# A seven-product feed-forward on one Trainium2 core: the second weight sum moved, and three of eleven units given a seventh pair

## The chip, the core and the metric

The kernel runs on one core of a Trainium2 chip. The engines are named as in the profile: PE (TensorE, matrix products), PEld (its weight loads), DVE (VectorE), ACT (ScalarE), POOL (GpSimd) and SP (SyncE, which here only issues DMAs). Every engine runs its own instruction list in order; semaphores tie the lists together. The metric is the device time of one execution in microseconds (us), lower is better.

## The reference

A trunk of two residual layers on 256 tokens of width 2048, in float32: attention and feed-forward, then a gated linear recurrence and feed-forward. The change lies in the two feed-forwards:

```python
def swiglu(h, w_gate, w_up, w_down):
    return (jax.nn.silu(h @ w_gate) * (h @ w_up)) @ w_down

x = x + mixer(rms_norm(x, norm_mix[i]))
x = x + swiglu(rms_norm(x, norm_ffn[i]), ffn_w_gate[i], ffn_w_up[i], ffn_w_down[i])
```

`w_gate` and `w_up` are 2048 x 5632, `w_down` is 5632 x 2048.

## The kernel before

**Split precision.** Each float32 operand is held as two fp32r halves: `hi`, a cast made by ACT, and `lo`, the remainder (the value less `hi`) made by DVE. A product is three matmuls of 512 columns (`product`, lines L323, L324, L326: hi by hi, lo by hi, hi by lo). So every 512 KB of weights that arrives costs ACT one cast and DVE one subtraction before PE can use it. `behind("cast", ...)` and `behind("rest", ...)` tie all these casts on ACT and all remainders on DVE into the order in which the program wrote them.

**Units and pairs.** A feed-forward is cut into 11 units of 512 hidden features. In a unit the 2048 rows of `w_gate` and `w_up` come as eight **pairs**, each of 256 rows (two blocks of 128) of gate and of up. A pair is a 2 x 2 block product: tokens in two halves, rows in two blocks, gate and up as the two columns. It is done either plainly, by `load_half` twice and `wide` (8 products, 24 matmuls), or by **seven products** (`load_seven`, 21 matmuls), which needs sums of weight blocks: with b11, b21 (gate) and b12, b22 (up), t1 = b11 + b12, t2 = t1 + b22, t3 = t2 - b11, t4 = t2 + b21. t1 is made by an accumulating DMA on POOL's queue (L176), or on DVE (L174) where three plain loads went ahead; the others are made on DVE (L169) and cast and subtracted in turn (L170, L171). The sums are made in place: t2 over b22, t3 over b11, t4 over b21. The token side needs such sums as well; `Norm.form` makes them once for each feed-forward and each pair that any unit does by seven products.

`SEVEN` names the six pairs so treated (0, 1, 2, 4, 5, 6, counted from 0); `FEWER` gives the first three units fewer. The texts count units and pairs from 1: usually pairs 1, 2, 3, 5, 6, 7 are done by seven products, pairs 4 and 8 plainly. After each of the units 3 to 10 come two column groups of the down projection of an earlier part, 96 matmuls, in `wide_project`; ACT takes their sums out of PSUM with a scale (`form`, L818, the **scaled copies**), and POOL adds them to the residual stream by DMA.

**What sets the order.** PE's order is the program's. The order on DVE, ACT, POOL and SP is made by a list scheduler within the ties that `behind`, `follow`, `ahead` and `held` add. At a unit's end DVE combines the PSUM banks (`sums`, L770 to L773, and L791, L794), ACT applies SiLU, DVE multiplies (L795) and transposes in 32 x 32 blocks (L408), and ACT puts the blocks in their place (L416, sixteen copies). These **turn copies** are split into four lots of four, held in the list `tail`; each `load_seven` of the next unit pops one lot between the casts of its loaded weights and those of its sums. The last lot brings the cast and remainder of the finished features (`whole`, L801 and L802). `parted` ties the second group's scaled copies behind the sums' casts.

**Buffers.** Weight tiles go round 8 `raw` buffers (`landing`), their halves round 7 `hi` and 7 `lo` buffers (`parts`); `ohi` and `olo`, the halves of t2, have two buffers each.

Of the kernel before, what the change touches and what calls it, by code (L numbers as in the profile page):

```python
# [12 lines left out]
F32 = mybir.dt.float32  # L13
F32R = mybir.dt.float32r
AF = mybir.ActivationFunctionType
ALU = mybir.AluOpType
AX = mybir.AxisListType

P = 128
# [8 lines left out]
PARTS = [8, 8, 8, 8, 12]  # L28
UNIT = 4
SEVEN = (0, 1, 2, 4, 5, 6)  # L30
FEWER = {0: (0, 5, 6), 1: (4, 5, 6), 2: (1, 4, 5, 6)}
HALF = 8
CHUNK = HALF * P
WIDE = 512
RING = 5
MORE = 2
RAWS = 3
SCRATCH = 8192
NW = D // WIDE
COMMON = {"ssq", "nm", "nr", "rsq_s"}  # L40
EPS = 1e-6
# [19 lines left out]
PK = {}  # L61
# [13 lines left out]
def trunk(ctx, tc, w, out):  # L75
    nc = tc.nc
    act, dve, pool, pe, sync = nc.scalar, nc.vector, nc.gpsimd, nc.tensor, nc.sync

    cst = ctx.enter_context(tc.tile_pool(name="cst", bufs=1))
# [13 lines left out]
    def tmp(tag, shape=(P, S), dt=F32, bufs=2):  # L93
        pl = tp if tag in COMMON else scope[-1]
        return pl.tile(list(shape), dt, tag=tag, name=nm(tag), bufs=bufs)


    newest = {}

    def follow(i, j):  # L100
        tc.add_manual_dep(
            i.ins, j.ins.name,
            mybir.DependencyInfo(mybir.DependencyClass.NoSync, mybir.DependencyReason.DATA),
            reason="order",
        )


    ring, held, ft, ahead, tail, parted = [0], [], [], [], [], []

    def parts(shape):  # L110
        n = ring[0] = (ring[0] + 1) % (RING + MORE)
        if ft and n >= RING:
            return [scope[-1].tile(shape, F32R, tag="x" + t, name=nm(t), bufs=MORE) for t in ("hi", "lo")]
        return [wp.tile(shape, F32R, tag=t, name=nm(t), bufs=RING) for t in ("hi", "lo")]
# [39 lines left out]
    def load_seven(srcs, soon):  # L154
        raw = [landing([P, 2, WIDE]) for _ in range(2)]
        for r, src in zip(raw, srcs):
            sync.dma_start(out=r, in_=src)
        (b11, b21), (t1, b22) = ([r[:, j, :] for j in range(2)] for r in raw)
        got = {}

        def two(src, names):
            hi, lo = parts([P, 2, WIDE])
            behind("cast", act.copy(hi, src))  # L163
            behind("rest", dve.tensor_tensor(lo, src, hi[:].bitcast(F32), ALU.subtract))  # L164
            for j, name in enumerate(names):
                got[name] = hi[:, j, :], lo[:, j, :]

        def combine(o, x, y, op, hi, lo):
            behind("rest", dve.tensor_tensor(o, x, y, op))  # L169
            behind("cast", act.copy(hi, o))  # L170
            return lambda: behind("rest", dve.tensor_tensor(lo, o, hi.bitcast(F32), ALU.subtract))  # L171

        if soon:
            behind("rest", dve.tensor_tensor(t1, b11, t1, ALU.add))  # L174
        else:
            pool.dma_start(out=t1, in_=b11, accum_op=ALU.add)  # L176
        two(raw[0], ("b11", "b21"))
        two(raw[1], ("t1", "b22"))
        if tail:
            tail.pop(0)()  # L180
        one = [tmp(t, (P, WIDE), F32R) for t in ("ohi", "olo")]
        hi, lo = parts([P, 2, WIDE])
        got["t2"] = tuple(one)
        got["t3"], got["t4"] = ((hi[:, j, :], lo[:, j, :]) for j in range(2))
        t2 = b22
        rests = [
            combine(t2, t1, b22, ALU.add, *got["t2"]),
            combine(b11, t2, b11, ALU.subtract, *got["t3"]),
            combine(b21, t2, b21, ALU.add, *got["t4"]),
        ]  # L190
        while parted:
            follow(parted.pop(), newest["cast"])
        for rest in rests:
            rest()
        return got
# [34 lines left out]
    for b in range(-1, NBLK):  # L230
        xin = range(2 * b + 2, 2 * b + 4) if b + 1 < NBLK else []
        yin = range(KT + 2 * b, KT + 2 * b + 2) if b >= 0 else []
        both = [halves(w["w_in"][c]) for c in (*xin, *yin)]
# [33 lines left out]
    def later(delay, fn):  # L267
        waiting.append((clock[0] + delay, fn))
# [117 lines left out]
    pk = cst.tile([P, PKW], F32, tag="pk", name="pk")  # L386
# [2 lines left out]
    scope.append(ap)  # L389
    xq = [ap.tile([P, 4, S], F32, tag=f"xq{k}", name=f"xq{k}", bufs=1) for k in range(KT // 4)]  # L390
    cn = ap.tile([P, 2 * S], F32, tag="cn", name="cn", bufs=1)
    ones = cst.tile([P, P], F32, tag="ones", name="ones")
    act.dma_start(out=pk[:, :PK0], in_=w["pk"][:, :PK0])
    pool.memset(ones, 1.0)
    idle = ps_m.tile([P, P], F32, tag="pm", name=nm("pm"))
# [28 lines left out]
    class Norm:  # L424
# [30 lines left out]
        def turn(self, g, engines):  # L455
            t = turn_blocks(x_tm[:, :, g * WIDE : (g + 1) * WIDE], engines)
            for k in range(4):
                self.scale(t[:, k, :])
            for i in range(2):
                if self.g[0] == "norm_ffn" and 2 * g + i in SEVEN:  # L460
                    self.form(2 * g + i, t[:, 2 * i : 2 * i + 2, :])

        def form(self, c, src):
            v, t = (tmp("form", (P, 2 * S)).rearrange("p (a b) -> p a b", a=n) for n in (2, 4))
            for j in range(2):
                act.activation(v[:, j, :], src[:, j, :], AF.Copy, scale=col(self.g[0], self.g[1] + 2 * c + j))
            (a11, a21), (a12, a22) = ([v[:, j, a * P : (a + 1) * P] for a in range(2)] for j in range(2))
            for i, x, y, op in (
                (0, a21, a22, ALU.subtract), (1, a11, a21, ALU.subtract),
                (2, t[:, 0, :], a11, ALU.subtract), (3, a12, t[:, 2, :], ALU.add),  # L470
            ):
                pool.tensor_tensor(t[:, i, :], x, y, op)
            hi, lo = (tmp(f"f{n}", (P, 4, P), F32R, bufs=len(SEVEN)) for n in "hl")
            act.copy(hi, t)
            dve.tensor_tensor(lo, t, hi[:].bitcast(F32), ALU.subtract)
            self.forms[c] = [(hi[:, i, :], lo[:, i, :]) for i in range(4)]
# [234 lines left out]
    for h in range(NQ):  # L711
        attend(h, project(n0.xs), o_t[h])

    cs = cst.tile([P, 32], F32, tag="cs", name="cs")
    ncs = cst.tile([P, 32], F32, tag="ncs", name="ncs")

    def decay_constants():
        lam = pk[:, PK["lam"] : PK["lam"] + 32]
        e, s, s2, q = (tmp(f"lr{i}", (P, 32), bufs=1) for i in range(4))
        dve.tensor_scalar(s, lam, -1.0, None, ALU.mult)  # L720
        dve.tensor_tensor(e, lam, s, ALU.max)
        table_act(e, e, AF.Exp, scale=-1.0)
        dve.tensor_scalar(s2, e, 2.0, None, ALU.add)
        dve.reciprocal(s2, s2)
        dve.tensor_tensor(e, e, s2, ALU.mult)
        dve.tensor_tensor(s2, e, e, ALU.mult)
        dve.tensor_scalar(q, s2, 2.0 / 15.0, 2.0 / 13.0, ALU.mult, ALU.add)
        for d in (11, 9, 7, 5, 3, 1):
            dve.tensor_tensor(q, q, s2, ALU.mult)
            dve.tensor_scalar(q, q, 2.0 / d, None, ALU.add)  # L730
        dve.tensor_tensor(q, q, e, ALU.mult)
        dve.scalar_tensor_tensor(q, s, 0.0, q, ALU.max, ALU.add)
        dve.tensor_scalar(cs, q, LRU_C, None, ALU.mult)
        dve.tensor_scalar(ncs, q, -LRU_C, None, ALU.mult)
# [15 lines left out]
    def ffn(norm, nxt):  # L750
# [60 lines left out]
        ends = np.cumsum(PARTS) // UNIT  # L811
        for what, i in ffn_plan():
            if what == "unit":
                hid[int(np.searchsorted(ends, i, "right"))] += unit(FEWER.get(i, SEVEN), 0 < i < ends[-1] - 1, (act,) if i < ends[-1] - 1 else (act, dve), i < ends[0])
            else:
                for a, acc in enumerate(wide_project(hid[i[0]], PARTS[i[0]], bank)):
                    t = tmp("form", (P, WIDE))
                    m = act.activation(t, acc, AF.Copy, scale=norm.r[:, a : a + 1])  # L818
                    if i[1] % 2:
                        parted.append(m)  # L820
                    pool.dma_start(out=x_tm[:, a, i[1] * WIDE : (i[1] + 1) * WIDE], in_=t, accum_op=ALU.add)
# [221 lines left out]
```

## Time and profile before

| what | value |
|---|---|
| runs shown, median (lowest to highest) | 1952.95 us (1952.37 to 1953.81), three runs |
| the profiled execution | 1952.89 us, of which the span from first to last instruction is 1951.1 us |
| attention in full run, 120 to 200 us | PE busy 80.00 of 80.00 us, DVE 65.65, ACT 61.27 |
| recurrence in full run, 1000 to 1100 us | PE busy 100.00 of 100.00 us, DVE 93.91, ACT 90.31 |
| second feed-forward, 1600 to 1700 us | PE busy 100.00 of 100.00 us, DVE 97.12, ACT 75.64 |
| last stretch, 1900 to 1952 us | PE busy 46.97 of 52.00 us |

The page's first part gives each engine's busy time over the span. The view by windows cuts this into stretches, so that stages with different limits can be told apart; the number behind "x" is the count of instructions. The view of waits sums, for each engine and line, how long it stood until which other engine released it. The timeline gives start and duration of single instructions; a row with x2 stands for two in succession. The first feed-forward takes about 266 to 904 us of the span, the second about 1263 to 1900 us.

### The profile page before, as it was taken

Reading aid. Unit: us, or ns where it says so; the run is one execution under the profiler, and the core shown is the slowest. Engines: PE = TensorE matmul, PEld = TensorE weight load, DVE = VectorE, ACT = ScalarE, POOL = GpSimd, SP = SyncE. Lnnn points to the kernel's source line nnn. Section 1 sums busy time; section 2 is a strip of 40 time slices with the busy share of each in tenths; the row PEclk is TensorE's granted clock in tenths of the full one; section 3 lists DMA queues with packets and bytes.
Section 4 is the critical chain, followed back from the end, with each engine's and each line's share of the span. In section 5 each row is a group of like instructions: output and inputs, shape, how many; then the busy total and the mean of one; then the engine's idle time right before and its main releaser. Section 6 shows DMA issues by size and latency. Waiting matters only on the chain.

```text
span 1951.1 us, 27630 instructions
## 1 busy us (share of the span) xinstructions
PE 1938.0 (99%) x9224; PEld 1624.0 (83%) x9224; DVE 1768.6 (91%) x2417; ACT 1448.3 (74%) x2358; POOL 401.3 (21%) x497
## 2 busy tenths in 40 slices
PE   9999999999999999999999999999999999999999
PEld 8898888788888888888899998887888888888887
DVE  7878698999999999998799997898999999999993
ACT  7677686777777777777698887866778776787772
POOL 0442250011101111010465450520101111011100
PEclk9999999999999999999999999999999999999999
DMA  8434746698878978787365556555878888788872
GB/s 328 156 127 152 248 158 197 196 272 236 248 233 243 262 240 246 235 244 246 126 223 188 189 164 245 175 194 174 253 236 248 245 248 253 231 246 251 246 257 86
DMA packets 131727, 426.42 MB, mean 219 GB/s; under 512 B 14720, under 2 KB 14976, under 8 KB 131584
## 3 DMA queue, kind: packets, MB, share of 16 engines
q1 hardware_dynamic: 108944, 383.21, 58.0%
q0 software_dynamic: 22496, 41.43, 11.9%
q8 instruction: 72, 1.18, 0.2%
q14 instruction: 71, 0.58, 0.1%
q10 hardware_dynamic: 144, 0.02, 0.0%
HBM read 382.13 MB, written 2.10 MB: 197 GB/s over the span
## 4 chain that ended last, share of the span: by engine, by line
PE 92%; DVE 4%; ACT 1%; issue 1%; DMA 1%; POOL 0%; SPq 0%; ACTq 0%; DVEq 0%; POOLq 0%
PE acc L326 14%; PE acc L323 14%; PE acc L324 14%; PE pm L326 11%; PE pm L323 11%; PE pm L324 11%; PE acc L294 8%; PE acc L292 4%; PE pm L306 1%; PE pm L307 1%; PE pm L305 1%; DVE lo L146 1%; ACT hi L145 1%; DVE lo L164 0%; DMA raw<-in_w_in_dram 0%
## 5 line engine op out<-in xcount | busy, mean ns | idle before, releaser
L146 DVE TENSOR_TENSOR lo<-raw,hi 128x1024 fp32r<-128x1024 f32 (+1 forms) x474 | 574.5, 1240 | 77.1 <-ACT hi L145 75.3
L145 ACT CAST hi<-raw 128x1024 fp32r<-128x1024 f32 (+1 forms) x474 | 478.4, 1045 | 116.5 <-PE acc L324 72.1
L326 PE MATMUL acc<-lo,xg 128*128 128x512 f32 x744 | 290.9, 391 | 2.0 <-DVE lo L146 1.8
L323 PE MATMUL acc<-hi,xg 128*128 128x512 f32 x744 | 290.0, 390 | 0.0
L324 PE MATMUL acc<-hi,xg 128*128 128x512 f32 x744 | 289.6, 389 | 0.0
L164 DVE TENSOR_TENSOR lo<-raw,hi 128x1024 fp32r<-128x1024 f32 x232 | 275.0, 1217 | 6.5 <-ACT hi L163 3.8
L294 PE MATMUL acc<-xg,hi 128*128 128x512 f32 x832 | 271.7, 397 | 0.6 <-ACT hi L145 0.6
L163 ACT CAST hi<-raw 128x1024 fp32r<-128x1024 f32 x232 | 234.6, 1048 | 41.0 <-issue 14.4
L176 POOL DMA_DIRECT2D raw<-raw x90 | 77.7, 863 | 903.9 <-DVE raw L174 369.5
L323 PE MATMUL pm<-hi,act 128*128 128x512 f32 x512 | 199.2, 389 | 0.0
L324 PE MATMUL pm<-hi,act 128*128 128x512 f32 x512 | 199.2, 389 | 0.0
L326 PE MATMUL pm<-lo,act 128*128 128x512 f32 x512 | 199.2, 389 | 0.0
L416 ACT COPY two<-one 32x256 f32<-32x256 f32 x420 | 169.7, 404 | 24.7 <-DVE one L408 16.5
L292 PEld LDWEIGHTS acc<-xg,lo 128*128 128x128 f32 x832 | 156.3, 188 | 35.4 <-DVE lo L146 2.8
L323 PE MATMUL acc<-hi,act 128*128 128x512 f32 x448 | 174.9, 390 | 0.4 <-DVE two L794 0.4
L326 PE MATMUL acc<-lo,act 128*128 128x512 f32 x448 | 174.4, 389 | 0.0
L324 PE MATMUL acc<-hi,act 128*128 128x512 f32 x448 | 174.4, 389 | 0.0
L292 PE MATMUL acc<-xg,lo 128*128 128x256 f32 x832 | 171.8, 281 | 1.2 <-DVE lo L146 1.2
L326 PEld LDWEIGHTS acc<-lo,xg 128*128 128x128 f32 x744 | 139.7, 188 | 34.1 <-DVE lo L146 5.4
L324 PEld LDWEIGHTS acc<-hi,xg 128*128 128x128 f32 x744 | 139.7, 188 | 29.2
L323 PEld LDWEIGHTS acc<-hi,xg 128*128 128x128 f32 x744 | 139.7, 188 | 28.6
L170 ACT CAST hi<-raw 128x512 fp32r<-128x512 f32 x232 | 137.1, 622 | 32.8 <-DVE raw L169 31.8
(221 smaller groups left out, 3852.1 us busy)
## 6 DMA issues: line engine op xcount, KB each, us to landing
raw<-in_w_gate_dram SPq DMA_DIRECT2D x176, 512.0 KB, 4.6
raw<-in_w_up_dram SPq DMA_DIRECT2D x176, 512.0 KB, 5.5
raw<-in_w_down_dram SPq DMA_DIRECT2D x176, 512.0 KB, 4.4
raw<-in_w_in_dram SPq DMA_DIRECT2D x64, 512.0 KB, 4.4
raw<-raw POOLq DMA_DIRECT2D x90, 256.0 KB, 5.8
raw<-in_w_q_dram SPq DMA_DIRECT2D x32, 512.0 KB, 3.8
raw<-in_w_o_dram SPq DMA_DIRECT2D x32, 512.0 KB, 4.2
x<-form POOLq DMA_DIRECT2D x64, 256.0 KB, 6.7
```

Source lines behind the costliest of these rows:

```text
L145: behind("cast", act.copy(hi[:, sl], raw[:, sl]))
L146: behind("rest", dve.tensor_tensor(lo[:, sl], raw[:, sl], hi[:, sl].bitcast(F32), ALU.subtract))
L163: behind("cast", act.copy(hi, src))
L164: behind("rest", dve.tensor_tensor(lo, src, hi[:].bitcast(F32), ALU.subtract))
L170: behind("cast", act.copy(hi, o))
L176: pool.dma_start(out=t1, in_=b11, accum_op=ALU.add)
L292: pe.matmul(acc[:, S:], w, xs[k][:, :S], start=False, stop=stop)
L294: pe.matmul(acc, w, xs[k], start=(k == 0), stop=stop)
L323: pe.matmul(o, xh, wh, start=start, stop=False)
L324: pe.matmul(o, xl, wh, start=False, stop=False)
L326: pe.matmul(o, xh, wl, start=False, stop=stop)
L416: m = (eng.copy if eng is act else eng.tensor_copy)(to[:, :, :, i, :], of[:, :, :, j, :])
```

## The change

The core of the diff; left out are renamed uses and two lines that only follow from it.

```diff
-FEWER = {0: (0, 5, 6), 1: (4, 5, 6), 2: (1, 4, 5, 6)}
+CHOSEN = {0: (0, 5, 6), 1: (4, 5, 6), 2: (1, 4, 5, 6)}
+MANY = tuple(range(7))
+CHOSEN.update({i: MANY for i in (4, 7, 10)})
...
-SCRATCH = 8192
+SCRATCH = 4096
...
-    ring, held, ft, ahead, tail, parted = [0], [], [], [], [], []
+    ring, held, ft, ahead, tail, parted, skip = [0], [], [], [], [], [], []
...
         two(raw[0], ("b11", "b21"))
+        got["t2"] = hi, lo = tuple(tmp(t, (P, WIDE), F32R) for t in ("ohi", "olo"))
+        t2 = tmp("sum", (P, WIDE), bufs=1)
+        behind("rest", dve.tensor_tensor(t2, t1, b22, ALU.add))
         two(raw[1], ("t1", "b22"))
-        if tail:
+        behind("cast", act.copy(hi, t2))
+        if tail and not skip:
             tail.pop(0)()
-        one = [tmp(t, (P, WIDE), F32R) for t in ("ohi", "olo")]
-        hi, lo = parts([P, 2, WIDE])
-        got["t2"] = tuple(one)
-        got["t3"], got["t4"] = ((hi[:, j, :], lo[:, j, :]) for j in range(2))
-        t2 = b22
+        skip.clear()
+        both = parts([P, 2, WIDE])
+        got["t3"], got["t4"] = (tuple(t[:, j, :] for t in both) for j in range(2))
         rests = [
-            combine(t2, t1, b22, ALU.add, *got["t2"]),
+            lambda: behind("rest", dve.tensor_tensor(lo, t2, hi[:].bitcast(F32), ALU.subtract)),
             combine(b11, t2, b11, ALU.subtract, *got["t3"]),
             combine(b21, t2, b21, ALU.add, *got["t4"]),
         ]
         while parted:
-            follow(parted.pop(), newest["cast"])
+            skip.append(parted.pop())
+            follow(skip[-1], newest["cast"])
...
-    ones = cst.tile([P, P], F32, tag="ones", name="ones")
+    ones = ap.tile([P, P], F32, tag="ones", name="ones", bufs=1)
...
-                if self.g[0] == "norm_ffn" and 2 * g + i in SEVEN:
+                if self.g[0] == "norm_ffn" and 2 * g + i in MANY:
...
-    cs = cst.tile([P, 32], F32, tag="cs", name="cs")
+    cs = pk[:, PK["lam"] : PK["lam"] + 32]
...
     scope.append(rt.enter_context(tc.tile_pool(name="rp", bufs=2)))
+    ones = tmp("ones", (P, P), bufs=1)
+    pool.memset(ones, 1.0)
     later(SPREAD, nr.spread)
```

So t2 gets a tile of its own, `sum`, and is added before the remainder of the up tile; its cast stands ahead of a lot of turn copies; a pair whose predecessor tied scaled copies gets no such lot; units 5, 8 and 11 do pair 4 by seven products too (six pairs more in the two feed-forwards, with token sums for pair 4); and some SBUF is freed: `ones` is written a second time for the recurrence, `cs` takes the place of its input, and the scratch for POOL's DMAs is halved.

**DVE, fifth unit of the first feed-forward, pairs 3 and 4.** Before; `lo` from a `raw` of 1024 columns is a remainder of loaded weights, `raw<-raw` a sum in place, and the last two rows are pair 4, done plainly:

```order
L164 TENSOR_TENSOR lo_5132<-raw_5126,hi_5131 128x1024
L164 TENSOR_TENSOR lo_5136<-raw_5127,hi_5135 128x1024
L169 TENSOR_TENSOR raw_5127<-raw_5127 128x512
L169 TENSOR_TENSOR raw_5126<-raw_5127,raw_5126 128x512 x2
L171 TENSOR_TENSOR olo_5144<-raw_5127,ohi_5143 128x512
L171 TENSOR_TENSOR lo_5146<-raw_5126,hi_5145 128x512 x2
L146 TENSOR_TENSOR lo_5179<-raw_5177,hi_5178 128x1024
L146 TENSOR_TENSOR lo_5197<-raw_5195,hi_5196 128x1024
```

The same place with the change (line numbers are the changed kernel's):

```order
L166 TENSOR_TENSOR lo_5157<-raw_5151,hi_5156 128x1024
L182 TENSOR_TENSOR sum_5162<-raw_5152 128x512
L166 TENSOR_TENSOR lo_5165<-raw_5152,hi_5164 128x1024
L171 TENSOR_TENSOR raw_5151<-sum_5162,raw_5151 128x512 x2
L191 TENSOR_TENSOR olo_5161<-sum_5162,ohi_5160 128x512
L173 TENSOR_TENSOR lo_5174<-raw_5151,hi_5173 128x512 x2
L166 TENSOR_TENSOR lo_5209<-raw_5203,hi_5208 128x1024
L182 TENSOR_TENSOR sum_5214<-raw_5204 128x512
L166 TENSOR_TENSOR lo_5217<-raw_5204,hi_5216 128x1024
L171 TENSOR_TENSOR raw_5203<-sum_5214,raw_5203 128x512 x2
L191 TENSOR_TENSOR olo_5213<-sum_5214,ohi_5212 128x512
L173 TENSOR_TENSOR lo_5226<-raw_5203,hi_5225 128x512 x2
```

The second sum has moved between the two wide remainders, and pair 4 has six narrow (512-column) rows more.

**ACT, the same unit, pairs 2 and 3.** Before; `hi` from 1024 columns is a cast of loaded weights, `two<-one` four turn copies, `form<-pm` a scaled copy, `ohi` the cast of t2, and `hi` from 512 columns the casts of t3 and t4:

```order
L163 CAST hi_5080<-raw_5075 128x1024
L163 CAST hi_5084<-raw_5076 128x1024
L416 COPY two_4466<-one_4852 32x8x32 x4
L818 ACTIVATE form_5008<-pm_4934,nr_3161 128x512
L818 ACTIVATE form_5011<-pm_4935,nr_3161 128x512
L170 CAST ohi_5092<-raw_5076 128x512
L170 CAST hi_5094<-raw_5075 128x512 x2
L163 CAST hi_5131<-raw_5126 128x1024
L163 CAST hi_5135<-raw_5127 128x1024
L416 COPY two_4466<-one_4852 32x8x32 x4
L170 CAST ohi_5143<-raw_5127 128x512
L170 CAST hi_5145<-raw_5126 128x512 x2
```

With the change:

```order
L165 CAST hi_5108<-raw_5103 128x1024
L165 CAST hi_5116<-raw_5104 128x1024
L823 ACTIVATE form_5035<-pm_4961,nr_3172 128x512
L184 CAST ohi_5112<-sum_5114 128x512
L823 ACTIVATE form_5038<-pm_4962,nr_3172 128x512
L172 CAST hi_5121<-raw_5103 128x512 x2
L165 CAST hi_5156<-raw_5151 128x1024
L165 CAST hi_5164<-raw_5152 128x1024
L184 CAST ohi_5160<-sum_5162 128x512
L421 COPY two_4487<-one_4879 32x8x32 x4
L172 CAST hi_5173<-raw_5151 128x512 x2
```

Pair 2 has lost its turn copies and has the cast of t2 between the scaled copies; in pair 3 the turn copies now stand behind the cast of t2 and ahead of the casts of t3 and t4. The lots of turn copies fall to pairs 1, 3, 4 and 5 of this unit (before: 1, 2, 3 and 5).

More of the change, by code (lines that the diff above doesn't have):

```diff
@@ L223, in ffn_order @@
             both = [(w[f"w_gate{l}"][i, c], w[f"w_up{l}"][i, c]) for c in range(KT // 2)]
-            seq += sum(([b] if c in (FEWER.get(i, SEVEN)) else list(b) for c, b in enumerate(both)), [])
+            seq += sum(([b] if c in (CHOSEN.get(i, SEVEN)) else list(b) for c, b in enumerate(both)), [])
         return seq + out_order(w[f"w_down{l}_{len(PARTS) - 1}"], UNIT // 2)
@@ L472, in form @@
                 pool.tensor_tensor(t[:, i, :], x, y, op)
-            hi, lo = (tmp(f"f{n}", (P, 4, P), F32R, bufs=len(SEVEN)) for n in "hl")
+            hi, lo = (tmp(f"f{n}", (P, 4, P), F32R, bufs=len(MANY)) for n in "hl")
             act.copy(hi, t)
@@ L712, in trunk @@
         attend(h, project(n0.xs), o_t[h])
-    cs = cst.tile([P, 32], F32, tag="cs", name="cs")
+    cs = pk[:, PK["lam"] : PK["lam"] + 32]
     ncs = cst.tile([P, 32], F32, tag="ncs", name="ncs")
     def decay_constants():
-        lam = pk[:, PK["lam"] : PK["lam"] + 32]
+        lam = cs
         e, s, s2, q = (tmp(f"lr{i}", (P, 32), bufs=1) for i in range(4))
@@ L813, in ffn @@
             if what == "unit":
-                hid[int(np.searchsorted(ends, i, "right"))] += unit(FEWER.get(i, SEVEN), 0 < i < ends[-1] - 1, (act,) if i < ends[-1] - 1 else (act, dve), i < ends[0])
+                hid[int(np.searchsorted(ends, i, "right"))] += unit(CHOSEN.get(i, SEVEN), 0 < i < ends[-1] - 1, (act,) if i < ends[-1] - 1 else (act, dve), i < ends[0])
             else:
```

## The prediction

> **What bounds the kernel now.** First the page's busy times, then the windows of the first feed-forward, then PE's waits.
>
> ```profile
> span 1951.1 us, 27630 instructions
> PE   1938.0 (99%) x9224; PEld 1624.0 (83%) x9224; DVE 1768.6 (91%) x2417; ACT 1448.3 (74%) x2358; POOL 401.3 (21%) x497
> ...
> 200.00:300.00 100.00, 100.00 (x443) 82.81 (x442) 82.24 (x103) 73.29 (x126) 39.42 (x53) 1.00 0.61 198
> 330.00:400.00 70.00, 67.84 (x292) 53.80 (x291) 68.22 (x85) 50.73 (x73) 1.71 (x2) 1.00 0.63 204
> 400.00:500.00 100.00, 100.00 (x443) 82.84 (x442) 97.46 (x118) 74.32 (x112) 15.63 (x18) 1.00 0.88 255
> 500.00:600.00 100.00, 100.00 (x442) 82.82 (x442) 97.43 (x119) 73.37 (x105) 11.65 (x14) 1.00 0.81 246
> ...
> PE pm L323 <- ACT ohi L170: 2.4, 2, 1.2
> PE acc L326 <- DVE lo L146: 1.8, 3, 0.8
> PE pm L493 <- DVE dg L492: 0.7, 1, 0.7
> PE acc L323 <- DVE two L794: 0.4, 2, 0.2
> ```
>
> PE sets the time: it is busy without a break in the units from 400 us on, at the full granted clock (1.00). But DVE, busy 97% there, is close behind. So a matmul less saves its time only while DVE still delivers early enough; the question is how early it delivers now. The waits for `ohi` (2.4 us in all) lie at the start of the two feed-forwards (the row of 330 to 400 us).
>
> PE's pace is the distance of two like matmuls, the first to use the cast of t2 in pair 1, in the fifth and in the sixth unit:
>
> ```profile
> 480.12 0.39 PE L323 MATMUL pm<-ohi,fh 128*128 128x512 f32 x1
> ...
> 541.32 0.39 PE L323 MATMUL pm<-ohi,fh 128*128 128x512 f32 x1
> ```
>
> A period is 61.20 us and holds 6 x 21 + 2 x 24 + 96 = 270 matmuls: 0.2267 us each.
>
> How early DVE delivers is read from the timeline of the fifth unit, one of the three to be changed:
>
> ```profile
> 473.55 1.22 DVE L164 TENSOR_TENSOR lo<-raw,hi 128x1024 fp32r<-128x1024 f32 x1
> ...
> 478.87 0.69 DVE L171 TENSOR_TENSOR olo<-raw,ohi 128x512 fp32r<-128x512 f32 x1 [0.91 <-ACT ohi L170]
> 479.48 1.29 DVE L171 TENSOR_TENSOR lo<-raw,hi 128x512 fp32r<-128x512 f32 x2
> 480.86 2.36 DVE L164 TENSOR_TENSOR lo<-raw,hi 128x1024 fp32r<-128x1024 f32 x2
> 483.25 0.69 DVE L169 TENSOR_TENSOR raw<-raw 128x512 f32<-128x512 f32 x1
> 483.98 1.29 DVE L169 TENSOR_TENSOR raw<-raw,raw 128x512 f32<-128x512 f32 x2
> 485.19 0.68 DVE L171 TENSOR_TENSOR olo<-raw,ohi 128x512 fp32r<-128x512 f32 x1
> 485.79 1.29 DVE L171 TENSOR_TENSOR lo<-raw,hi 128x512 fp32r<-128x512 f32 x2
> 487.00 2.35 DVE L146 TENSOR_TENSOR lo<-raw,hi 128x1024 fp32r<-128x1024 f32 x2
> 489.27 2.35 DVE L164 TENSOR_TENSOR lo<-raw,hi 128x1024 fp32r<-128x1024 f32 x2
> ...
> 507.13 0.68 DVE L171 TENSOR_TENSOR olo<-raw,ohi 128x512 fp32r<-128x512 f32 x1
> ...
> 508.94 1.22 DVE L146 TENSOR_TENSOR lo<-raw,hi 128x1024 fp32r<-128x1024 f32 x1
> 510.30 0.69 DVE L770 TENSOR_TENSOR one<-one,pm 128x512 f32<-128x512 f32 x1
> ...
> 480.57 0.39 PE L326 MATMUL pm<-olo,fh 128*128 128x512 f32 x1
> ...
> 509.81 0.39 PE L326 MATMUL pm<-olo,fh 128*128 128x512 f32 x1
> ...
> 511.85 0.39 PE L326 MATMUL acc<-lo,xg 128*128 128x512 f32 x1
> ```
>
> In pair 7 `olo` is ready at 507.81 and used at 509.81: 2.00 us early. The first `lo` of pair 8 is ready at 510.16 and used at 511.85: **1.69 us** early. In pair 2, whose `olo` is used 21 matmuls behind 480.57, at 485.33, `olo` was ready at 479.56: 5.8 us early. The lead melts along a unit, because a seven-product pair takes DVE 487.00 - 480.86 = 6.14 us and PE 21 x 0.2267 = 4.76, and it is rebuilt in pair 4 (DVE 2.27, PE 24 x 0.2267 = 5.44) and in the down groups. The 1.69 us at the end of a unit is what the change can spend.
>
> **The change part by part.**
>
> *PE.* Three matmuls less in each of six pairs: 0.68 us a pair, 4.1 us in all, if PE never waits.
>
> *DVE, pair 4 by seven products.* Two wide remainders stand 489.27 - 487.00 = 2.27 us for both; a narrow step 485.79 - 485.19 = 0.60. Six narrow steps more: 3.63 us (at 0.605, two in 1.21).
>
> *DVE, the second sum moved.* Now that sum stands 2.39 us behind the first of two wide remainders, 0.12 more than 2.27, and the next sum 0.73 behind it (483.98 - 483.25), 0.13 more than 0.60: each works in place on what the step ahead has just read or written. In the new order a wide remainder lies between them. I take 0.25 us off: a pair's bare price is 5.90 us.
>
> The Trainium skill's page "VectorE: DVE Perf Modes", section "The DRAIN you can't avoid", says that a DVE op holds the next one until its pipe is empty, whether or not a semaphore stands between. By that rule the 0.25 would not be there to win, and the sum would be the third rival's. The rows speak against it: dependent sums stand 0.73 apart, others 0.60.
>
> *ACT, turn copies behind the cast of t2.* Now ACT works through them ahead of that cast:
>
> ```profile
> 478.74 1.14 ACT L170 CAST hi<-raw 128x512 fp32r<-128x512 f32 x2
> 479.78 2.00 ACT L163 CAST hi<-raw 128x1024 fp32r<-128x1024 f32 x2
> 481.80 1.65 ACT L416 COPY two<-one 32x256 f32<-32x256 f32 x4
> 484.06 0.62 ACT L170 CAST ohi<-raw 128x512 fp32r<-128x512 f32 x1 [0.61 <-DVE raw L169]
> ...
> L163 ACT CAST hi<-raw 128x1024 fp32r<-128x1024 f32 x232 | 234.6, 1048 | 41.0 <-issue 14.4
> ```
>
> In the new order ACT has, from the end of the second sum to the end of the next pair's first cast: the cast of t2 (half of 479.78 - 478.74, 0.52), the copies 1.65, the casts of t3 and t4 1.04, a wide cast 1.05, and two hand-overs at 0.04 (as from 483.94 to 483.98), 4.34 us. DVE in that time has one wide and five narrow steps, 1.135 + 3.03 less 0.08 of overlap, 4.08. So the next pair's first remainder waits 0.26 us for its cast, with every later step of DVE queued behind it, and a pair with turn copies costs 6.16, as much as now. Much hangs on this: the new place of the sum wins 0.25 us, and in four pairs of a unit the copies take it back. `sum` has one buffer, but its last reader stands earlier on DVE, so it adds no wait.
>
> *The ledger of a changed unit*, as lateness of DVE at the first `lo` of pair 8. Pair 1: the transpose comes after the sum, so the copies start later, and the casts of t3 and t4 behind them make DVE wait 0.6, then 0.26; less 0.25: **+0.6**. Pair 2 takes 480.86 - 473.55 = 7.31 now, 0.91 of it the wait for `ohi` behind copies; without its lot of copies 5.90, and I leave 0.2 for the scaled copies, which still wait for PE's group: **-1.2**. Pair 3: 0. Pair 4: **+3.63 + 0.26**. Pair 5 (copies and `whole`): 0. Pairs 6 and 7: **-0.5**. Together +2.8. PE wants the weights 0.68 earlier: 3.5. Lead 1.69: PE stands about **1.8 us** in each changed unit, and gains 0.68: +1.15 net, 6.9 us for six.
>
> Bounds: with none of the new waits on ACT the pairs give 3.63 - 5 x 0.25 - 1.4 = 1.0, and 1.0 + 0.68 is just the lead: no stall, -0.68 a unit. With no gain in any pair the stall is 3.63 + 0.26 + 0.6 + 0.68 - 1.69 = 3.5, +2.8 a unit. I take the middle value, since its terms follow from rows.
>
> *The units between.* PE has no wait there that could go. A unit in which DVE starts late makes it up from the same gains, without pair 4's cost, before the next changed unit comes.
>
> *The end of each feed-forward.* Unit 11 is a changed one, and the groups behind it need the PSUM banks that DVE empties:
>
> ```profile
> 884.35 0.68 DVE L794 TENSOR_TENSOR two<-acc,two 128x512 f32<-128x512 f32 x1
> ...
> 884.49 0.39 PE L326 MATMUL acc<-lo,act 128*128 128x512 f32 x1
> 885.09 0.50 PE L323 MATMUL acc<-hi,act 128*128 128x512 f32 x1 [0.21 <-DVE two L794]
> ```
>
> PE already loses 0.60 - 0.23 = 0.37 us there. DVE arrives with the whole lead spent, 1.69 us later against PE, of which 0.5 us of its waits around L770 (510.30 rather than 510.08) and L791 is made up: **+1.2 us**, twice: 2.4.
>
> *The rest.*
>
> ```profile
> raw<-raw POOLq DMA_DIRECT2D x90, 256.0 KB, 5.8
> ```
>
> Six accumulating DMAs more, 5.8 us to landing: the eight `raw` buffers let loads run up to four pairs, some 24 us of DVE, ahead, which hides them. The token sums for pair 4 (two forms) are made beside the output projection, where DVE is 82% and ACT 73% busy (200 to 300 us); `ones` again is one memset on POOL, at a place where PE waits 0.7 us for DVE anyway; `cs` moves no work. I count 0 (up to 1 us for all). Halved scratch: no row shows POOL's DMAs short of it; 0.
>
> *The sum.* 6.9 + 2.4 = +9.3 on the profiled execution's 1952.89 (0.06 us under the median of 1952.95): **1962.2 us**, 0.5% slower.
>
> **The rivals.**
>
> 1. *DVE keeps up* (the other side). If ACT's casts are early enough and the 0.26 and 0.6 do not arise, the ledger is 0, all 4.1 us are won, and the waits for `ohi` at the start may halve: 1952.9 - 4.1 - 1.2 = 1947.6. For it: ACT is only 74% busy. Against it: the 0.26 follows from in-order work, not from a shortage. It decides at a ledger of 1.0 before pair 8. Chance 0.12.
> 2. *Half of the new waits*: stall 0.9, +0.2 a unit, 0.6 at each end: 1952.9 + 1.4 + 1.2 = 1955.5, no measurable change. Chance 0.15.
> 3. *The moved sum wins nothing on DVE*: in pairs 2, 6 and 7 the 0.25 stays: stall 2.55, +1.9 a unit: 1952.9 + 11.2 + 2.4 = 1966.5. This is what the DRAIN rule above would make. Chance 0.07.
> 4. *Lateness outlives the two units between*, or the six new accumulating DMAs land late: the next changed unit then finds no lead, 1.69 us more in four of six: 1962.2 + 6.8 = 1969. Chance 0.06. That the change does not do what it says is excluded by the rows of the order.
>
> **How the numbers follow.** The forecast, 1957 to 1966, has 0.60. From these: faster by over 0.2% (3.9 us, about what a measurement of this kernel tells from none; below 1949.0) 0.12; within it 0.15; slower 0.73. The range reaches from 1950 into the second rival's side to 1967.5 over the third; outside are the first and the fourth, 0.18.
>
> **What would show it.** Right: in units 5, 8 and 11 PE has new waits on `olo` or `lo`, in pieces below 1 us from pair 6 to pair 8, some 1.8 us a unit, none in the units between; the wait for L794 grows past 1 us; DVE waits 0.2 to 0.3 us for L163 behind lots of turn copies; narrow sums stand 0.60 apart. Wrong: PE at 100% in the windows of the changed units, or its new waits in other units. Should PE wait only at the feed-forwards' ends, the ledger of the pairs was too dark.

## The result, and the profile after

The changed kernel takes **1980.44 us** in the median of four runs (1978.71 to 1981.79), before beside it 1953.24 us. The ratio is 1.0139, 95% interval 1.0122 to 1.0157: slower by 27 us, where 9.3 were forecast. The profiled spans are 1976.9 and 1951.1 us; the sums below are made on that difference, 25.8 us.

The page's first part and the windows that answer to those of before (the columns are stretch, then busy time and count of PE, PEld, DVE, ACT, POOL, then granted clock, DMA share, GB/s):

```profile
span 1976.9 us, 27695 instructions
PE 1950.2 (99%) x9206; PEld 1617.3 (82%) x9206; DVE 1780.9 (90%) x2455; ACT 1457.4 (74%) x2382; POOL 415.0 (21%) x512
```
```profile
200.00:300.00 100.00, 96.39 (x422) 79.24 (x421) 74.95 (x94) 69.97 (x122) 39.43 (x54) 0.99 0.59 193
300.00:330.00 30.00, 29.65 (x127) 24.10 (x126) 28.01 (x36) 19.82 (x29) 4.96 (x6) 0.96 0.68 224
...
400.00:500.00 100.00, 100.00 (x443) 82.82 (x442) 96.87 (x120) 73.06 (x109) 16.48 (x19) 1.00 0.88 255
500.00:600.00 100.00, 99.36 (x431) 79.90 (x430) 97.98 (x120) 72.56 (x102) 10.88 (x13) 1.00 0.79 241
```

Read the counts, not the busy time: PE shows 99.36 of 100 us busy from 500 to 600 us, yet did 431 matmuls where before did 442. A matmul is shown as 0.39 us long with a modelled end, while the next one usually begins 0.23 us behind it, so a wait of up to 0.16 us does not show as idle time. From 200 to 300 us, the end of the output projection and the start of the feed-forward, 21 matmuls are missing, and there no pair has been added.

PE's waits, longest in total first (engine, tile and line, what it waited for: us, times, longest):

```profile
PE pm L329 <- DVE fl L480: 4.2, 4, 1.7
PE pm L328 <- ACT fh L479: 3.2, 2, 2.1
PE pm L331 <- DVE olo L191: 2.9, 10, 0.8
PE acc L331 <- DVE lo L148: 2.4, 4, 0.8
PE acc L328 <- DVE two L799: 2.3, 2, 1.2
...
PE pm L331 <- DVE lo L166: 1.0, 6, 0.2
PE acc L331 <- DVE lo L173: 1.0, 2, 0.6
```

The forecast named the waits for `olo` and `lo` in small pieces and that for L799 (before L794). The two largest, `fh` and `fl`, the halves of the token forms, it did not name.

Where the time goes is read from one mark in every pair, the first matmul that uses the cast of t2, set against the same mark of before. Rows of after, the first pair of units 4, 5 and 6 of the first feed-forward, then of units 1 and 4 of the second:

```profile
424.41 0.39 PE L328 MATMUL pm<-ohi,fh 128*128 128x512 f32 x1
485.61 0.39 PE L328 MATMUL pm<-ohi,fh 128*128 128x512 f32 x1
548.90 0.39 PE L328 MATMUL pm<-ohi,fh 128*128 128x512 f32 x1
1279.35 0.39 PE L328 MATMUL pm<-ohi,fh 128*128 128x512 f32 x1
1433.41 0.39 PE L328 MATMUL pm<-ohi,fh 128*128 128x512 f32 x1
```

Before has 418.92, 480.12, 541.32, 1266.10 and 1415.91. So PE is 5.49 us late when unit 4 begins; unit 4 itself takes 61.20 us as before; the changed unit 5 takes 63.29, 2.09 more; and the second feed-forward's start loses 17.50 - 13.25 = 4.25. Summed over the program:

| stage | forecast | measured |
|---|---|---|
| starts of the feed-forwards, to unit 4 | 0 | 5.5 + 4.2 = 9.7 |
| six changed units | 6.9 | 14.2 (2.0 to 2.1 each, two of them 2.8 and 3.2) |
| units between | 0 | 0.5 |
| ends, recurrence | 2.4 | 1.4 |
| sum | 9.3 | 25.8 |

**A changed unit.** DVE in the fifth unit: the first remainder of pairs 4, 5, 6, 7 and 8, and L807, the remainder of the activations:

```profile
492.23 1.23 DVE L166 TENSOR_TENSOR lo<-raw,hi 128x1024 fp32r<-128x1024 f32 x1 [0.18 <-ACT hi L165]
...
498.61 1.23 DVE L166 TENSOR_TENSOR lo<-raw,hi 128x1024 fp32r<-128x1024 f32 x1 [0.17 <-ACT hi L165]
...
504.47 1.23 DVE L807 TENSOR_TENSOR act<-two,act 128x1024 fp32r<-128x1024 f32 x1 [0.26 <-ACT act L806]
...
506.21 1.22 DVE L166 TENSOR_TENSOR lo<-raw,hi 128x1024 fp32r<-128x1024 f32 x1
...
512.10 1.22 DVE L166 TENSOR_TENSOR lo<-raw,hi 128x1024 fp32r<-128x1024 f32 x1
...
517.98 1.22 DVE L148 TENSOR_TENSOR lo<-raw,hi 128x1024 fp32r<-128x1024 f32 x1
```

A pair without copies takes 512.10 - 506.21 = 5.89 us (forecast 5.90), one with copies 498.61 - 492.23 = **6.38** (forecast 6.16). Against PE, which is 5.49 us later than before, DVE begins pair 5 at +3.85 us (498.61 - 5.49 - 489.27) and pair 8 at +3.55 (517.98 - 5.49 - 508.94); forecast was +2.8 for pair 8. ACT in pair 3 shows why:

```profile
487.78 0.62 ACT L184 CAST ohi<-sum 128x512 fp32r<-128x512 f32 x1 [1.02 <-DVE sum L182]
488.43 1.65 ACT L421 COPY two<-one 32x256 f32<-32x256 f32 x4
490.10 1.14 ACT L172 CAST hi<-raw 128x512 fp32r<-128x512 f32 x2
491.15 2.00 ACT L165 CAST hi<-raw 128x1024 fp32r<-128x1024 f32 x2
```

DVE's second sum ends at 487.67, the next pair's first cast at 492.20 (half of the last row): 4.56 us with the hand-over to DVE at 492.23, where the forecast had 4.34. The cast of t2 takes 0.65 us to the start of the copies behind it, and not the 0.52 that lie between two like casts, and the hand-over to it is 0.11 (487.67 to 487.78). DVE has 4.08 us of work in that time, so it waits about 0.2 us more than forecast in each pair with copies.

**A feed-forward's start.** In the first one PE stands twice, 2 us apart (PE, then ACT, DVE and POOL on the form ahead of it):

```profile
296.08 0.50 PE L328 MATMUL pm<-hi,fh 128*128 128x512 f32 x1 [2.07 <-ACT fh L479]
298.12 0.50 PE L329 MATMUL pm<-hi,fl 128*128 128x512 f32 x1 [1.54 <-DVE fl L480]
...
299.37 0.63 PE L331 MATMUL acc<-lo,fh 128*128 128x512 f32 x1
299.80 0.63 PE L328 MATMUL pm<-ohi,fh 128*128 128x512 f32 x1
...
284.70 0.62 ACT L479 CAST fh<-form 128x512 fp32r<-128x512 f32 x1 [5.46 <-POOL form L477]
...
285.36 0.69 DVE L480 TENSOR_TENSOR fl<-form,fh 128x512 fp32r<-128x512 f32 x1 [2.50 <-ACT fh L479]
...
279.54 4.06 POOL L477 TENSOR_TENSOR form<-form 128x128 f32<-128x128 f32 x2 [0.93 <-DVE fl L480]
```

Unit 1 uses pairs 1, 6 and 7, so the forms of pairs 6 and 7 are wanted at once. The form for pair 4 is made ahead of them, in the same `form` buffers and the same POOL queue. The rows of ACT, DVE and POOL above are those of pair 5's form: POOL begins its sums when DVE has read the form of pair 4 (`fl`), ACT stands 5.46 us until they are done, and everything behind that cast waits too, the cast of pair 6's form among it.

Not all of the loss is waiting. Behind the two waits eight matmuls stand 0.43 us apart instead of 0.227, at a lower granted clock: 8 x 0.2 = 1.6 us. The last section comes back to this; it bears on several experiments.

### The profile page after: what moved, and what is told of

Same layout as the page of the kernel before. It is cut to its first block, busy times and chain, and to the rows that moved or that the text cites. A ratio compares the mean times of both kernels' runs of the same rounds, so it can differ in the third digit from the quotient of the medians.

```text
span 1976.9 us, 27695 instructions
## 1 busy us (share of the span) xinstructions
PE 1950.2 (99%) x9206; PEld 1617.3 (82%) x9206; DVE 1780.9 (90%) x2455; ACT 1457.4 (74%) x2382; POOL 415.0 (21%) x512
## 4 chain that ended last, share of the span: by engine, by line
PE 82%; DVE 10%; issue 4%; ACT 2%; POOL 1%; DMA 1%; SPq 0%; DVEq 0%; ACTq 0%; POOLq 0%
PE acc L331 12%; PE acc L328 12%; PE acc L329 12%; PE pm L329 10%; PE pm L331 10%; PE pm L328 10%; PE acc L299 8%; PE acc L297 4%; DVE lo L148 2%; DVE raw L171 1%; PE pm L311 1%; PE pm L312 1%; PE pm L310 1%; DVE lo L166 1%; POOL form L477 1%
## 5 line engine op out<-in xcount | busy, mean ns | idle before, releaser
L148 DVE TENSOR_TENSOR lo<-raw,hi 128x1024 fp32r<-128x1024 f32 (+1 forms) x462 | 562.4, 1245 | 81.2 <-ACT hi L147 80.2
L147 ACT CAST hi<-raw 128x1024 fp32r<-128x1024 f32 (+1 forms) x462 | 466.2, 1045 | 97.6 <-PE acc L329 71.0
L166 DVE TENSOR_TENSOR lo<-raw,hi 128x1024 fp32r<-128x1024 f32 x244 | 298.2, 1222 | 9.4 <-ACT hi L165 8.6
L165 ACT CAST hi<-raw 128x1024 fp32r<-128x1024 f32 x244 | 246.9, 1048 | 46.8 <-PE pm L329 19.9
L331 PE MATMUL acc<-lo,xg 128*128 128x512 f32 x708 | 277.9, 392 | 3.4 <-DVE lo L148 2.4
L328 PE MATMUL acc<-hi,xg 128*128 128x512 f32 x708 | 276.4, 390 | 0.2 <-DVE x L352 0.2
L329 PE MATMUL acc<-hi,xg 128*128 128x512 f32 x708 | 275.8, 390 | 0.0
L173 DVE TENSOR_TENSOR lo<-raw,hi 128x512 fp32r<-128x512 f32 x244 | 160.1, 690 | 18.1 <-ACT hi L172 13.2
L172 ACT CAST hi<-raw 128x512 fp32r<-128x512 f32 x244 | 143.2, 619 | 37.5 <-DVE raw L171 35.2
L331 PEld LDWEIGHTS acc<-lo,xg 128*128 128x128 f32 x708 | 132.9, 188 | 37.8 <-DVE lo L148 8.2
L171 DVE TENSOR_TENSOR raw<-sum,raw 128x512 f32<-128x512 f32 x244 | 156.7, 683 | 0.0
```

Source lines behind the costliest of these rows:

```text
L147: behind("cast", act.copy(hi[:, sl], raw[:, sl]))
L148: behind("rest", dve.tensor_tensor(lo[:, sl], raw[:, sl], hi[:, sl].bitcast(F32), ALU.subtract))
L328: pe.matmul(o, xh, wh, start=start, stop=False)
L329: pe.matmul(o, xl, wh, start=False, stop=False)
L331: pe.matmul(o, xh, wl, start=False, stop=stop)
```

## The experiments

All against before on the same chip: 1952.77 us beside the first four, 1953.01 beside the next four, 1953.27 beside the last. The stage columns give the us by which each profiled execution falls behind before (to unit 4; units 4 to 11 as far as pair 7 of unit 11; from there to the second feed-forward; then the same three again), read from the mark above.

| run | median us | ratio, 95% interval | start 1 | units 1 | between | start 2 | units 2 | end |
|---|---|---|---|---|---|---|---|---|
| the changed kernel | 1980.44 | 1.0122 to 1.0157 | 5.5 | 6.5 | 1.2 | 4.2 | 6.6 | 1.7 |
| e1_order_only | 1957.55 | 1.0013 to 1.0032 | 3.7 | 0.0 | 1.3 | -0.5 | 0.0 | 0.3 |
| e2_form_only | 1965.68 | 1.0050 to 1.0080 | 5.9 | 0.0 | 1.6 | 3.9 | 1.6 | 0.8 |
| e3_form_late | 1983.47 | 1.0138 to 1.0169 | 1.8 | 14.6 | 0.4 | 1.4 | 10.9 | 1.7 |
| e4_old_order | 1976.01 | 1.0103 to 1.0137 | 4.4 | 5.5 | 0.9 | 4.1 | 5.6 | 2.3 |
| e5_copies_first | 1973.20 | 1.0082 to 1.0115 | 7.6 | 1.9 | 0.2 | 7.9 | 2.8 | 1.7 |
| e6_form_pool | 1973.04 | 1.0090 to 1.0121 | 2.5 | 7.4 | 0.4 | 1.7 | 6.5 | 1.7 |
| e7_both | 1964.02 | 1.0044 to 1.0074 | 3.7 | 1.4 | 0.9 | 1.9 | 1.3 | 1.9 |
| e8_memory_only | 1952.78 | 0.9990 to 1.0009 | 0.5 | 0.0 | 0.1 | 0.1 | 0.1 | 0.0 |
| e9_order_later | 1958.83 | 1.0015 to 1.0037 | -0.2 | 1.6 | 5.2 | -0.2 | 0.4 | 1.5 |
| e10_all_three | 1965.33 | 1.0039 to 1.0073 | 3.6 | 3.9 | 0.5 | 2.2 | 2.4 | 2.9 |
| e11_whole_pool | 1980.72 | 1.0125 to 1.0155 | 3.4 | 11.6 | 0.4 | 1.9 | 10.6 | 1.7 |
| e12_no_skip | 1985.18 | 1.0149 to 1.0179 | 5.7 | 8.8 | 0.4 | 6.8 | 8.6 | 1.7 |

**e1_order_only** and **e2_form_only** take the change apart:

```diff
-CHOSEN.update({i: MANY for i in (4, 7, 10)})
-MANY = tuple(range(7))
+MANY = SEVEN
```

(e2 has only the first line of it: the seventh form is made and not used.)

> The changed kernel with six pairs by seven products in units 5, 8 and 11 again and without the token form for pair 4; the sum in its own tile, the place of the copies and the smaller tiles stay. Theory A (the loss comes from the seventh pairs and from the seventh token form, the new order of a pair costs nothing): 1951 us (1949.5 to 1953.5), PE without a wait in units 4 to 12, waits for fh and fl at the feed-forwards' starts gone, wait for L799 at the ends 0.2 to 0.4 us. Theory B (the copies behind the cast of t2 hold DVE up by themselves): 1957 or more, with PE waits on olo or lo at the ends of units. Theory C (the new order was worth something by itself): below 1949.

> As e1_order_only, but the token form for pair 4 is made (and never used). Theory A (the seventh form delays the forms of pairs 6 and 7, which unit 1 needs at once): 8 to 10 us above e1_order_only, so about 1960, nearly all of it before unit 4 of each feed-forward, with PE waits for fh and fl of some 7 us. Rival (the forms were late for another cause, such as the loads of the new pairs or the smaller DMA scratch): as e1_order_only, within 1.5 us.

Without the seventh pairs PE loses nothing in units 4 to 11: the waits there belong to the pairs. But e1 is 4.8 us slower than before. That is the time of theory B without its mechanism, since no wait came at the ends of units: 3.7 of it lie at the first feed-forward's start, nothing at the second. Which step is late first there is not shown. The cast of t2 waits for its sum only once, 0.85 us at 293.90, while a form's cast already comes 4 us later than in before ahead of that (281.11 for 277.04, with a wait of 3.31 us for POOL's sums). PE's waits in e1 between 240 and 420 us:

```profile
PE acc L330 <- DVE lo L147: 1.3, 3, 0.8
PE pm L327 <- ACT fh L478: 1.1, 1, 1.1
PE pm L330 <- DVE olo L190: 0.8, 1, 0.8
PE pm L328 <- DVE fl L479: 0.5, 1, 0.5
```

The form made for nothing adds 8.1 us (1965.68 - 1957.55), as theory A had it, though less of it before unit 4 than it said: in the profiled executions 2.2 at the first start, 4.5 at the second and 1.6 in the unit behind that.

**e3_form_late** makes the form for pair 4 at the start of unit 4:

```diff
-                if self.g[0] == "norm_ffn" and 2 * g + i in MANY:
+                if self.g[0] == "norm_ffn" and 2 * g + i in SEVEN:
...
+                if i == 3:
+                    norm.form(3, None)
```

> The changed kernel, with the token form for pair 4 made by POOL at the start of unit 4 (from the hi and lo of the block, so without ACT's two scaled copies) instead of among the others. Theory A: no PE wait for fh or fl, units 5, 8 and 11 as in the changed kernel (each 2.1 us longer than in before): 1980.4 less 9.5 = 1971 (1968.5 to 1973). Rival (the forms are late whatever their number, because POOL also makes the turn copies): within 2 us of 1980.

A miss, by 12 us. The starts do fall, to 1.8 and 1.4 us; the loss moved to unit 4. ACT and POOL there (`L483` is the cast of the form, `L481` its sums):

```profile
424.35 2.34 POOL L473 TENSOR_TENSOR form<-xg 128x256 f32<-128x256 f32 x2 [2.17 <-issue]
430.05 0.88 POOL L481 TENSOR_TENSOR form<-form 128x128 f32<-128x128 f32 x2 [3.36 <-DMA x<-form]
...
431.91 0.62 ACT L483 CAST fh<-form 128x512 fp32r<-128x512 f32 x1 [6.29 <-POOL form L481]
```

POOL waits 3.36 us for a `form` buffer that the transfer of a scaled copy still reads, and ACT waits 6.29 us for POOL with all later casts queued behind. Neither theory had priced the new place.

**e4_old_order** is the changed kernel with before's body of `load_seven`: t2 added in place behind both wide remainders, its cast behind the copies, no `skip`.

> The changed kernel with before's order inside a pair (the second sum in place, ohi cast behind the copies, copies wherever they are due); the seventh pairs, the seventh form and the smaller tiles stay. Theory A (the copies take back what the moved sum wins: a pair with copies takes DVE 6.38 us against 6.14, one without 5.89 against 6.12, pair 2 gains 1.2 once): a stall of 3.0 to 3.2 us in units 5, 8, 11 against 2.8, no extra lateness from the scaled copies; 1977 to 1984, within 4 us of the changed kernel. Rival 1 (the new order is what makes the seventh pairs nearly affordable): 1987 or more. Rival 2 (the new order is itself the loss): 1974 or less.

1976.0 us, 4.4 below the changed kernel, or 4.0 when each is taken against before beside it: at the edge of theory A's margin of 4. By the marks a changed unit loses 2.24 us with the old order and 2.10 with the new one: in the units the new order earns 0.14 us, about nothing, as theory A had it. What the old order wins lies elsewhere: 1.1 at the first start, and none of the two long delays behind scaled copies.

**e12_no_skip** drops the rule that keeps copies away from scaled copies:

```diff
-        if tail and not skip:
+        if tail:
```

> The changed kernel without the rule that a pair with scaled copies gets no turn copies. Theory A (the rule is nearly free: the four lots of copies only move by a pair): within 2.5 us of the changed kernel, 1978 to 1983. Rival 1 (the rule is worth its aim): 3 us or more above it, with DVE waiting for hi more than 1 us in the second pair of every unit. Rival 2 (the rule pushes copies and the activations' cast into the pairs behind pair 4, where the lead is spent): 3 us or more below it.

4.7 us slower: rival 1. A changed unit loses 3.1 us instead of 2.1, and units 4 to 11 account for 4.2 us of the profiled difference of 6.2. Another 2.6 us lie at the second start, where 13 matmuls run at the lower granted clock and none in the changed kernel. DVE and ACT in the second pair of unit 5:

```profile
483.25 1.65 ACT L421 COPY two<-one 32x256 f32<-32x256 f32 x4
484.93 0.69 ACT L823 ACTIVATE form<-pm,nr 128x512 f32<-128x512 f32 x1
485.51 1.13 ACT L172 CAST hi<-raw 128x512 fp32r<-128x512 f32 x2
...
486.15 1.29 DVE L173 TENSOR_TENSOR lo<-raw,hi 128x512 fp32r<-128x512 f32 x2 [2.02 <-ACT hi L172]
```

Copies and a scaled copy stand between the cast of t2 and those of t3 and t4, and DVE waits 2.02 us. The rule is a needed part of the new order.

**e5_copies_first**, **e6_form_pool** and **e7_both** (the two together) go for the two causes:

```diff
-        behind("cast", act.copy(hi, t2))
         if tail and not skip:
             tail.pop(0)()
         skip.clear()
+        behind("cast", act.copy(hi, t2))
```

e6 makes the form for pair 4 at the start of unit 2 by POOL alone: two sums of `hi` and `lo`, the four sums of the form, its cast and its remainder.

> The changed kernel with a turn's four copies ahead of the cast of t2 on ACT instead of behind it; all else stays. In e1_order_only to e4_old_order PE stood 2.78 us in a changed unit, of which the copies' place is to account for three pairs by 0.49 us (6.38 against 5.89 us) and 0.2 in the second pair. Theory A (the copies' place is the term that was sized too small): pairs with copies take DVE 5.9 us, the stall is 1.0 to 1.4 us, the kernel 9 to 11 us below the changed one, 1970 (1967.5 to 1972.5); the feed-forwards' starts stay as late as they are. Rival (the copies cost DVE the same anywhere in a pair, since a late cast of t2 then holds up the casts of t3 and t4): 1977 or more, with DVE waiting for ohi or hi 0.3 us or more a pair.

> The changed kernel with the token form for pair 4 made wholly by POOL (sums, cast and remainder) at the start of unit 2, so that no cast on ACT waits for it as in e3_form_late, where ACT stood 6.3 us for it and 4.2 us of the gain went. Theory A (the seventh form among the others delays those of pairs 6 and 7): 7 to 10 us below the changed kernel, 1970.5 to 1973.5, nearly no PE wait for fh and fl in the second feed-forward, 1 to 2 us left in the first (as in e1_order_only). Rival (POOL's work slows DVE, which has little lead in units 2 and 3): 1976 or more, with new PE waits for lo or olo in units 2 and 3.

> The edits of e5_copies_first and e6_form_pool together. Theory A (two causes in different places of the program): the sum of both gains, 1958 to 1963, with 0.3 to 0.7 us lost in each changed unit and the first feed-forward's start still late. Rival (one hides the other: a shorter start shifts the wait into the units): 1966 or more.

e5's fifth unit on DVE and ACT:

```profile
494.35 1.22 DVE L166 TENSOR_TENSOR lo<-raw,hi 128x1024 fp32r<-128x1024 f32 x1
...
500.23 1.22 DVE L166 TENSOR_TENSOR lo<-raw,hi 128x1024 fp32r<-128x1024 f32 x1
...
495.20 1.65 ACT L421 COPY two<-one 32x256 f32<-32x256 f32 x4
496.88 0.62 ACT L187 CAST ohi<-sum 128x512 fp32r<-128x512 f32 x1
497.94 1.23 ACT L172 CAST hi<-raw 128x512 fp32r<-128x512 f32 x2 [0.44 <-DVE raw L171]
```

A pair with copies now takes 500.23 - 494.35 = 5.88 us, no more than one without: the copies fit into a time in which ACT waited for the sum. The loss in units 4 to 11 falls from 13.2 to 4.7 us for both feed-forwards; PE still stands 1.2 to 1.8 us in a changed unit (units 5 and 8 of both), where 1.0 to 1.4 was expected. The median falls by 7.2 us and not by 9 to 11 (0.7 above the range), because the starts lose 5.7 more, which was not foreseen. Nearly all of that is the granted clock: 36 matmuls stand 0.43 us apart at the two starts, 8 in the changed kernel, and 28 x 0.2 = 5.6 us.

e6 falls by 7.4 us, as expected, in its profile by 5.6 at the starts; 1.6 of this is the eight slow matmuls, which are gone. Both together fall by 16.4, somewhat more than the sum of 14.6, to 1964.0, a us above the range; still 11 us slower than before.

**e8_memory_only** is before with the edits of `ones`, `cs` and `SCRATCH`.

> Before with the change's edits of memory alone: ones in two pools and set twice, cs in place of lam, half the DMA scratch. e1_order_only lost 3.8 us at the first feed-forward's start, 0.8 at its end and 0.5 behind it. Theory A (that comes from the new order of a pair, whose casts stand otherwise among the turns and forms): within 1 us of before, 1952 to 1954. Rival (POOL's transfers run short of scratch, or the second memset delays): 1955.5 or more.

No difference: the memory edits, counted at nothing, cost nothing.

**e9_order_later** and **e10_all_three** are e1 and e7 with before's body for the six pairs of units 1 and 2.

> e1_order_only (six pairs, no form for pair 4, 1957.6) with before's order inside the six pairs of units 1 and 2 of each feed-forward, whose loads are prepared among the turns and forms of the norm; the new order from unit 3 on. Theory A (what the new order loses, it loses there, by another place of its casts among ACT's turns and forms): nothing lost before unit 3, 1952 to 1954.5, the same as before. Rival (the loss at the first feed-forward's start comes from elsewhere): 1956.5 or more, with the waits for fh and fl as in e1_order_only.

> e7_both (copies ahead of the cast of t2, form for pair 4 by POOL; 1964.0) with before's order in the pairs of units 1 and 2. Theory A: the 2.8 to 3.7 us that e7_both lost at the first feed-forward's start go, 1960 to 1962; what is left is 0.5 to 1.0 us in each of six changed units, and the ends. Rival: 1963 or more.

In e9 the loss at the first start is gone (-0.2 against 3.7), so its place is shown. The time is not: 1958.8, with delays elsewhere, 1.6 us in units 7 to 10 and, in the profiled execution, 2.1 at one place of the recurrence. Its seven runs lie between 1956.2 and 1961.0. In e10 the mixture of orders brings new waits in units 2 and 3 (2.1, 1.1 and 1.1 us at the marks), and nothing is won. What the recurrence lost in e9 was not followed further and stays open.

**e11_whole_pool** gives L807, 1.14 us of DVE a unit, to POOL in units 2 to 10:

```diff
-                dve.tensor_tensor(t[:, :, S:], ht, t[:, :, :S].bitcast(F32), ALU.subtract)
+                (pool if beside else dve).tensor_tensor(t[:, :, S:], ht, t[:, :, :S].bitcast(F32), ALU.subtract)
```

> e10_all_three with the remainder of the activations (L807 in the changed kernel, 1.14 us of DVE in a unit and 0.26 us of waiting for its cast) computed by POOL in units 2 to 10. Theory A (the seventh pairs are paid by DVE's lateness alone, so work taken from DVE in the same unit comes back as PE time until the stall is gone): the stall of a changed unit falls from 1.2 to 1.7 us to 0.3 or less, units 5 and 8 then gain 0.4 to 0.7 us each; unit 11 gains less, since its remainder is that of unit 10. In all 4 to 7 us below e10_all_three. Rival (POOL's 5 us a unit slow DVE, or hold up POOL's transfers for the scaled copies): as e10_all_three within 2 us, or slower.

15 us slower than e10: the rival. The rows, from e11 (POOL and DVE) and then the same step of DVE in e10:

```profile
501.67 2.84 POOL L858 TENSOR_TENSOR act<-two,act 128x1024 fp32r<-128x1024 f32 x1 [1.11 <-ACT act L857]
...
502.16 3.49 DVE L173 TENSOR_TENSOR lo<-raw,hi 128x512 fp32r<-128x512 f32 x2
```
```profile
502.02 1.28 DVE L173 TENSOR_TENSOR lo<-raw,hi 128x512 fp32r<-128x512 f32 x2
```

While POOL works for 2.84 us, two narrow remainders of DVE take 3.49 us instead of 1.28. DVE is spared 1.14 us and loses 2.21. The other 17 of these subtractions on POOL show the same, with 1.8 to 2.2 us lost each. Theory A was not tested by this, since DVE did not get the time; that the stalls are paid in DVE's lateness rests on e1 and e5.

No version beat before. The best with seventh pairs is e7_both.

## Why the prediction was wrong

The direction was right, the size was not; the time lies outside the range. On the profiled executions 25.8 us were lost for 9.3: 9.7 at the starts for 0, 7.3 more than forecast in the changed units, 0.5 between them, and 1.0 less at the ends.

- **The failed step is "The rest".** "The token sums for pair 4 (two forms) are made beside the output projection, where DVE is 82% and ACT 73% busy (200 to 300 us)", counted at 0 with up to 1 us. The forms cost 8.1 us (e2 against e1), and the starts lose 5.6 us less when POOL makes them at unit 2 (e6). Room in an average over 100 us says nothing of who needs the next form and when: the extra form stands in the queues and buffers ahead of two that unit 1 uses at once.
- **That the new order costs time outside the changed units** was in no part of the forecast. e1: 4.8 us in the median, in its profile 3.7 at the first start; e9 shows that this comes from the pairs of units 1 and 2, though not by which step. Nor did the forecast have a term for the granted clock, which it took as 1.00 throughout; 1.6 us of the first start's loss are matmuls at a lower one.
- **The ledger of a changed unit** had the right mechanism and was short in one term, the hand-overs on ACT. Step by step, lateness at the next pair's first remainder: pair 1 +0.70 (forecast +0.6), pair 2 -1.21 (-1.2), pair 3 +0.25 (0), pair 4 +4.11 (+3.89), pair 5 +0.19 (0), pairs 6 and 7 -0.49 (-0.5). Sum +3.55 for +2.8. With 0.68 and less 1.69 that is a stall of 2.54; PE stood 2.77, and part of the rest is that a matmul behind a wait starts its successor 0.1 us late (516.92, then 517.25 in the trace, 0.33 where 0.23 is usual). Six times about 0.9 us are missing here (2.09 for 1.15), and with the two delays told below 7.3. e5 confirms it from the other side: with the copies ahead of the cast the term goes, and with it two thirds of the loss.
- **The moved sum wins 0.25 us a pair**: right, 5.89 against 6.12 to 6.14. The third rival falls with that; that its stall of 2.55 us lies near the measured 2.77 is luck, since the difference came from ACT and not from the sum. The DRAIN rule of the Trainium skill's page "VectorE: DVE Perf Modes", section "The DRAIN you can't avoid", taken as the prediction tells it, does not describe these rows, in which independent narrow steps of 0.69 us begin 0.60 apart; the same section also says that a next op which is not held starts earlier, and with that these rows agree. That the copies take the win back was forecast too; e4 shows that they do.
- **Units between**: right, no stall, but for 0.5 us. In two changed units (the eighth of the first feed-forward, the fifth of the second) a scaled copy waited and held ACT: 0.7 and 1.1 us more. In the first it waited 0.82 us for a transfer (`x<-form`) to free its buffer. In the second, 1.05 us, the view names PE; that it was the transfer as well is inferred from its landing, up to 8.4 us behind its issue at 1484.77, just ahead of the copy at 1493.28. These are the fourth rival in part, by a third cause.
- **Ends**: the wait for L799 (before L794) was to grow by 1.2 us at each end; it grew from 0.4 to 2.3 us for two, so by about 1.0 each, and with what else changed there 1.4 us were lost for 2.4. But the reason given, a unit 11 that spends the lead, is not the only one: in e1, where unit 11 has six pairs, the same wait is 1.5 us for two, in e8 0.5.

## What to carry to other kernels

An engine's average busy share does not show that an added step is free. Ask for each new instruction which buffer and which in-order queue it stands in, and what its successor there is due for; with an early consumer a few us away, one form more cost 2 us in one feed-forward and 6 in the other. And a small step on an engine with slack, put between two dependent casts, is paid by the engine that waits for the second cast: the same copies cost nothing ahead of the first one, in a time in which ACT waited for DVE.

## What the runs showed of the hardware

**POOL against DVE.** POOL's subtraction of two 128x1024 operands stretched two of DVE's from 1.28 to 3.49 us together (e11). The Trainium skill's page "GPSIMD Engine Reference", section "1. Specifications", says that POOL shares its way to SBUF with DVE and that they collide when DVE has two inputs there; these rows agree.

**The granted clock after short waits.** In the changed kernel, after the waits of 2.07 and 1.54 us at 296 and 298 us, with one matmul between them, eight matmuls stand 0.43 us apart (299.37, 299.80) where 0.227 is usual, and the windows show the lower clock:

```profile
290.00:300.00 10.00, 6.39 (x25) 4.72 (x24) 10.00 (x16) 7.82 (x17) 0.77 (x2) 0.94 0.33 105
300.00:310.00 10.00, 9.65 (x38) 7.55 (x37) 8.89 (x16) 8.60 (x13) 3.23 (x4) 0.88 0.64 210
```

That is some 1.6 us on top of the waits (8 x 0.2). In e5 a single wait of 1.80 us, 10 us behind the one before it, is followed by seven matmuls 0.43 us apart (369.04 to 371.60):

```profile
367.40 0.50 PE L328 MATMUL pm<-ohi,fh 128*128 128x512 f32 x1 [1.80 <-ACT ohi L187]
```
```profile
370.00:380.00 10.00, 10.00 (x41) 8.19 (x40) 10.00 (x13) 8.23 (x13) 1.71 (x2) 0.89 0.92 267
```

But a wait of 1.75 us in the second feed-forward of the changed kernel (1307.13) left the clock at 1.00, and so did two of 1.07 and 1.06 us in e6 (300.04 and 301.61). So the length of a wait alone does not decide it here, and what does is not shown. The Trainium skill's page "TensorE: Matmul & The Clock Gate", section "Part 1: The HAM clock gate", gives an idle window of about 3.4 us as what lowers the clock; none of these waits was that long, and one of 1.80 us was enough.
